# Attention value products as fp32 matmuls in two 64-column halves of TensorE's array

## The chip, the cores and the metric

The kernel runs on one core of a Trainium2 chip. The metric is the device time of one execution in microseconds. Before the change it is 2939.94 us, the median of three runs (2930.49 to 2944.06).

## The reference

One block of a model with 2048 tokens of width 1024, all in fp32. The input is normalised and modulated, projected by `w_in`, and mixed in two ways: an attention with three branches (compressed keys, selected blocks, a window of 512), and a recurrent mixer. Both outputs are normalised and projected back, and a gated feed-forward layer with a short convolution follows. The part that the change touches are the last lines of each attention branch:

```python
o_cmp = jnp.einsum('bgrsc,bgcd->bgrsd', p_cmp.astype(vc.dtype), vc)
...
p = _masked_softmax(jnp.einsum('bgrqd,bgqnd->bgrqn', qb, kg) * scale, mask)
return jnp.einsum('bgrqn,bgqnd->bgrqd', p.astype(vg.dtype), vg)
...
o_win = jnp.einsum('bgrnqk,bgnkd->bgrnqd', p_w.astype(vband.dtype), vband).reshape(B, G, R, S, DH)

g = jax.nn.sigmoid(zg + gate_b).reshape(B, S, G, R, N_BRANCH).transpose(0, 2, 3, 1, 4)
o = g[..., 0:1] * o_cmp + g[..., 1:2] * o_slc + g[..., 2:3] * o_win
```

There are 2 groups of keys and values, 4 query heads for each group, and 64 columns for each head. Queries go in blocks of 128.

## The kernel before

The kernel has three stages, each with pools of its own. The first projects the input in four chunks of 512 tokens, runs the recurrent mixer and writes queries, keys and values to DRAM. The second is the attention with the output projection. The third is the feed-forward layer, again in four chunks.

Most products are made in fp32r with both operands split: a tile is copied to an fp32r tile "h" (on ScalarE), and what is left of it goes into a second tile "l" (a subtraction, mostly on VectorE). A product is then three matmuls: h by h, h by l, l by h (`mm3`).

The attention stage runs over units, one for each query tile `i` (16 of them, in the order of `TILES`) and group `g`. `score_steps` makes the scores of the next unit and their exponentials, scaled by the gates; the tile `pc` holds the compressed and the window branch, the tiles `ps` the selected one. `value_steps` makes the value product of the current unit. Its work is a list of jobs, one for each tile of up to 128 keys: one job for the compressed keys (8 for each query tile up to the current one, so 8 to 128 rows), up to five for the window, and one for each tile of the selected branch, so that a unit has 3 to 22 jobs.

For each job, `flip` turns the four heads' weights around with four transposes on TensorE (line 785) into a PSUM tile `pt`, copies it to the fp32r tile `th` on ScalarE (line 786) and puts the rest into `tl` on VectorE (line 787). The values are stored split as well: 64 columns of "h" and 64 of "l" side by side, so one stationary tile of 128 columns. Two matmuls of 512 columns (lines 796 and 797) accumulate the job into `po`, whose lower 64 partitions collect the products with the values' h and whose upper 64 those with l:

```python
                pe.matmul(po, jobs[n][1], th, start=(n == 0), stop=False)
                pe.matmul(po, jobs[n][1], tl, start=False, stop=(n == N - 1))
```

`LOOK = 4` jobs are flipped ahead of the one that is multiplied. At the end of a unit the two halves of `po` are copied out on ScalarE (lines 805 and 806) and added on GpSimd (line 811).

Python's `weave` interleaves the steps of the value product, the next unit's scores and the previous tile's output projection (`project_steps`, line 131). The order of the instructions that the engines get is then set by the framework's scheduler, which goes by a timeline of its own (`schedule_with_timeline_sim=True`). Each engine runs its own stream in the order in which it was built, and waits on semaphores.

Two other places of the first stage speak of the same kind of arithmetic and matter for the trace: `ada_product` (line 173) multiplies in plain fp32 into four strips of 32 columns of the array, and the compressed keys (`pk`, line 545) are an fp32 product with 64 stationary columns and 256 streamed.

Of the kernel before, what the change touches and what calls it, by code (L numbers as in the profile page):

```python
# [9 lines left out]
F32 = mybir.dt.float32  # L10
F32R = mybir.dt.float32r
AF = mybir.ActivationFunctionType
OP = mybir.AluOpType
AX = mybir.AxisListType

P = 128
# [5 lines left out]
NQ = S // P  # L22
FF = 2816
NF = FF // P
G, R, DH = 2, 4, 64
# [18 lines left out]
LOOK = 4  # L44
# [9 lines left out]
def hymba_block(ctx, tc, x, vecs, rows, ada, w_in, w_v, lru_w, cmp_w1, cmp_w2, w_out, w_gu, w_dn,  # L54
# [6 lines left out]
    cst = ctx.enter_context(tc.tile_pool(name="cst", bufs=1))  # L61
# [2 lines left out]

    Q_d = dr.tile([G, DH, 2, R, S], F32, name="Q_d")
    K_d = dr.tile([2, G, 2, DH, S], F32, name="K_d")
    V_d = dr.tile([2, P, NQ, G, P], F32, name="V_d")
    C_d = dr.tile([2, G, 16, DH, S // 16], F32, name="C_d")
    L_d = dr.tile([P, 2, 4, S], F32, name="L_d")
    KC_d = dr.tile([G, 2, DH, P], F32, name="KC_d")  # L70
# [31 lines left out]
    gates = cst.tile([P, NQ, 24], F32, name="gates")  # L102

    rlru = cst.tile([P, NQ], F32, name="rlru")
    VC = cst.tile([P, G, P], F32R, name="VC")
    cvec = cst.tile([P, 8], F32, name="cvec")

    def reserve(pl, *tags):
# [111 lines left out]
    with tc.tile_pool(name="a", bufs=1, reuse_waits="tile") as pl, tc.tile_pool(name="ap", bufs=1, space=PSUM, reuse_waits="tile") as pp:  # L220
# [109 lines left out]
        def chunk(c, hT):  # L330
# [116 lines left out]
            def v_tiles(each=None):  # L447

                wv = [weights(c, "v", hf) for hf in range(2)]
                zv = [pp.tile([P, 280], F32, name=f"zv{c}_{t}", tag="z", bufs=4) for t in range(4)]  # L450
                for k in range(KT):
                    for t in range(4):
                        sl = slice(t * P, (t + 1) * P)
                        mm3(zv[t], [((hT[k][0][:, sl], hT[k][1][:, sl]),
                                     (wv[k // 4][0][:, k % 4], wv[k // 4][1][:, k % 4]))], 3 * k, 24)
                    if each:
                        each(k)
                for t in range(4):
                    ps = zv[t]
                    st = pl.tile([P, 4, 2, DH], F32R, name=f"vs{c}_{t}", tag="vst", bufs=2)  # L460
                    psv = ps[:, 0:256].rearrange("p (b d) -> p b d", d=DH)
                    act.activation(st[:, :, 0, :], psv, AF.Copy)
                    dve.tensor_tensor(st[:, :, 1, :], psv, st[:, :, 0, :].bitcast(F32), op=OP.subtract)
                    dve.tensor_tensor(gates[:, 4 * c + t, :], ps[:, 256:280], gb, op=OP.add)
                    sync.dma_start(V_d[:, :, 4 * c + t].rearrange("n p g d -> p n (g d)"),
                                   st.rearrange("p (n g) l d -> p n (g l d)", n=2).bitcast(F32))

            def zs(js):
                for j in js:
# [44 lines left out]
        def compress_step(q):  # L514
            n, qd = q // 4, q % 4
            if qd == 0:
                cs["ps"] = [pp.tile([P, G, NS], F32, name=f"ph{n}{hf}", tag="z", bufs=4) for hf in range(2)]
            wh, wl = weights(NCH - 1, "c", q)
            xh = pl.tile([P, 4, G, P], F32R, name=f"xbh{q}", tag="x", bufs=4)
            xl = pl.tile([P, 4, G, P], F32R, name=f"xbl{q}", tag="x", bufs=4)  # L520
            o = VEC["pos"][0] + 16 * n + 4 * qd
            pos = vec[:, o:o + 4].unsqueeze(2)
            a = int(qd < 2)
            for g in range(G):
                f = cs[q][g]
                dve.tensor_tensor(f[:, :, a:P], f[:, :, a:P], pos.to_broadcast([P, 4, P - a]), op=OP.add)
                act.activation(xh[:, :, g, :], f, AF.Copy)
                dve.tensor_tensor(xl[:, :, g, :], f, xh[:, :, g, :].bitcast(F32), op=OP.subtract)
            if q < 7:
                compress_load(q + 1)  # L530
            for hf in range(2):
                sl = slice(hf * P, (hf + 1) * P)
                mm3(cs["ps"][hf], [((wh[:, m, sl], wl[:, m, sl]), (xh[:, m], xl[:, m])) for m in range(4)], 12 * qd, 48)
            if qd < 3:
                return
            hid = []
            for hf in range(2):
                h = pl.tile([P, G, NS], F32, name=f"hid{n}{hf}", tag="xsh", bufs=2)
                dve.tensor_scalar(h, cs["ps"][hf], V("cb1", 2 * n + hf), None, op0=OP.add)
                gelu_tail(h, h, pl, [P, G, NS], "ge", True)  # L540
                hid.append(h)
            if n == 0:
                pk = pp.tile([DH, G * NS], F32, name="pk", tag="g", bufs=2)
                for hf in range(2):
                    pe.matmul(pk, w2[:, 0, hf, :], hid[hf].rearrange("p g s -> p (g s)"), start=(hf == 0), stop=(hf == 1))
                kf = pl.tile([DH, G, NS], F32, name="kf", tag="ge", bufs=2)
                b2 = V("cb2k")[0:DH]
                dve.tensor_scalar(kf, pk.rearrange("p (g s) -> p g s", g=G), b2, None, op0=OP.add)
                kh = pl.tile([DH, 2, G, NS], F32R, name="kh", tag="vst", bufs=2)
                act.activation(kh[:, 0], kf, AF.Copy)  # L550
                dve.tensor_tensor(kh[:, 1], kf, kh[:, 0].bitcast(F32), op=OP.subtract)
                for g in range(G):
                    act.dma_start(KC_d[g].rearrange("l d s -> d l s"), kh[:, :, g, :].bitcast(F32))
            else:
                pv = pp.tile([P, G, DH], F32, name="pv", tag="g", bufs=2)
                for g in range(G):
                    for hf in range(2):
                        pe.matmul(pv[:, g], hid[hf][:, g, :], w2[:, 1, hf, :], start=(hf == 0), stop=(hf == 1))
                vf = pl.tile([P, G, DH], F32, name="vf", tag="ge", bufs=2)
                dve.tensor_tensor(vf, pv, cb2v.unsqueeze(1).to_broadcast([P, G, DH]), op=OP.add)  # L560
                act.activation(VC[:, :, 0:DH], vf, AF.Copy)
                dve.tensor_tensor(VC[:, :, DH:P], vf, VC[:, :, 0:DH].bitcast(F32), op=OP.subtract)


        hT, wts = [], []
# [54 lines left out]
    with tc.tile_pool(name="t", bufs=1, reuse_waits="tile") as pl, tc.tile_pool(name="tp", bufs=1, space=PSUM, reuse_waits="tile") as pp:  # L620
        reserve(pp, ("s", 4096, 2), ("pt", 2048, 3), ("o", 2048, 1))
        reserve(pl, ("MW", 2560, 1), ("ci", 4 * CW, 2), ("Q", 4096, 2), ("K", 3072, 2), ("ks", 2048, 4),
                ("pc", 12288, 2), ("ps", 4096, 10), ("V", 2560, 2), ("vs", 2048, 3), ("pth", 2048, 4),
                ("ptl", 2048, 4))
        MW = pl.tile([P, 640], F32, name="MW", tag="MW", bufs=1)
        sync.dma_start(MW, mask_w)
        wo = {}
# [132 lines left out]
        def value_steps(i, g, u):  # L760

            nw, nk = u["nw"], i + 1
            Vt = pl.tile([P, 5, P], F32R, name=f"V{i}_{g}", tag="V", bufs=2)
            sync.dma_start(Vt[:, 0:nw].bitcast(F32), V_d[1, :, i + 1 - nw:i + 1, g, :])
            jobs = []
            C = 8 * nk
            jobs.append((lambda h: u["pc"][:, h, 0:C], VC[0:C, g, :]))
# [1 line left out]
                jobs.append((lambda h, j=j: u["pc"][:, h, C + j * P:C + (j + 1) * P], Vt[:, j, :]))  # L769
            for a in range(0, nk, 4):  # L770
                n = min(4, nk - a)
                vt = pl.tile([P, 4, P], F32R, name=f"vs{i}_{g}_{a}", tag="vs", bufs=3)
                sync.dma_start(vt[:, 0:n].bitcast(F32), V_d[0, :, a:a + n, g, :])
                for j in range(n):
                    jobs.append((lambda h, a=a, j=j: u["ph"][h][a // 8][:, (a % 8 + j) * P:(a % 8 + j + 1) * P], vt[:, j, :]))
            po = pp.tile([P, 512], F32, name=f"po{i}_{g}", tag="o", bufs=1)

            def flip(n):
                pt = pp.tile([P, 512], F32, name=f"pt{i}_{g}_{n}", tag="pt", bufs=3)
                th = pl.tile([P, 512], F32R, name=f"th{i}_{g}_{n}", tag="pth", bufs=4)  # L780
                tl = pl.tile([P, 512], F32R, name=f"tl{i}_{g}_{n}", tag="ptl", bufs=4)
                K = jobs[n][1].shape[0]
                pt, th, tl = pt[0:K], th[0:K], tl[0:K]
                for h in range(R):
                    pe.transpose(pt[:, h * P:(h + 1) * P], jobs[n][0](h), ident)  # L785
                act.activation(th, pt, AF.Copy)  # L786
                dve.tensor_tensor(tl, pt, th.bitcast(F32), op=OP.subtract)  # L787
                return th, tl

            N = len(jobs)  # L790
            fl = {n: flip(n) for n in range(min(LOOK, N))}
            for n in range(N):
                if n + LOOK < N:
                    fl[n + LOOK] = flip(n + LOOK)
                th, tl = fl.pop(n)
                pe.matmul(po, jobs[n][1], th, start=(n == 0), stop=False)
                pe.matmul(po, jobs[n][1], tl, start=False, stop=(n == N - 1))
                yield
            if g == 0:
                out_of[i] = (pl.tile([P, 2, 4, P], F32R, name=f"mx{i}", tag="mx", bufs=1),  # L800
                             pl.tile([P, 4, P], F32, name=f"sq{i}", tag="sq", bufs=1))
# [47 lines left out]
        def ffn_norm(i):  # L849
# [7 lines left out]
            yield  # L857
            for hf in range(2):
                pt = pp.tile([P, 4, P], F32, name=f"ft{i}{hf}", tag="pt", bufs=3)
                h = pl.tile([P, 4, P], F32R, name=f"fh{i}{hf}", tag="pth", bufs=4)  # L860
                l = pl.tile([P, 4, P], F32R, name=f"fl{i}{hf}", tag="ptl", bufs=4)
                f = pl.tile([P, 4, P], F32, name=f"ff{i}{hf}", tag="ps", bufs=10)
                for j in range(4):
                    k = 4 * hf + j
# [214 lines left out]
```

## Time and profile before

| | us |
|---|---|
| median of three runs | 2939.94 |
| profiled execution | 2934.73 |
| its span, first to last instruction | 2933.0 |
| TensorE (PE) busy in it | 2832.0 |
| VectorE (DVE) busy | 1694.0 |
| ScalarE (ACT) busy | 1497.8 |
| GpSimd (POOL) busy | 1322.3 |

The projection stage reaches to about 572 us, the attention stage from there to about 1437, the feed-forward stage from there to the end. Matmuls of a stream overlap, so that the sum of their durations is more than the time that they take; the distance from one start to the next is what one costs.

### The profile page before, as it was taken

The page shows a single profiled execution, that of the slowest core. Times are in us where ns is not written, and L with a number is a line of the kernel's source. Part 1 is how long each engine was busy: PE and PEld are TensorE (multiplying, and loading weights), DVE is VectorE, ACT ScalarE, POOL GpSimd, SP SyncE. Part 2 cuts the span into 40 slices and gives each one's busy share as a digit, 9 for nine tenths or more (in the row PEclk, how much of TensorE's full clock was granted, in tenths as well). Part 3 has the DMA queues.
Part 4 walks back from the last instruction along what each step waited for, and adds up shares of the span by engine and source line. Part 5 has one row for each costly group of instructions (what it writes and reads, how often), then busy time and mean ns, then how long its engine had stood idle before and what let it go on. Part 6 is the DMA issues. An engine that isn't in the chain of part 4 may idle for free. (4 is left out here: it accounts for less than half of the span.)

```text
span 2933.0 us, 40574 instructions
## 1 busy us (share of the span) xinstructions
PE 2832.0 (97%) x14436; PEld 2328.3 (79%) x14436; DVE 1694.0 (58%) x3149; ACT 1497.8 (51%) x2686; POOL 1322.3 (45%) x1392
## 2 busy tenths in 40 slices
PE   8999999889999899999999999999999999999998
PEld 6777778777778777888788888888887888888886
DVE  4656657776777888888566621666216662166610
ACT  5656566586777777777633333433334333233322
POOL 1111010166666556565344445544455444554444
PEclk9999999999999999999999999999999999999999
DMA  7576655764544434433533333433324333243332
GB/s 285 177 268 203 242 196 151 225 164 129 138 137 121 123 111 111 116 110 96 190 94 96 104 118 98 140 99 96 128 86 151 94 103 121 88 135 100 97 105 78
DMA packets 256617, 397.89 MB, mean 136 GB/s; under 512 B 41376, under 2 KB 168352, under 8 KB 256416
## 3 DMA queue, kind: packets, MB, share of 16 engines
q1 hardware_dynamic: 255808, 394.12, 43.5%
q8 instruction: 115, 1.88, 0.3%
q0 software_dynamic: 320, 1.05, 0.1%
q14 instruction: 86, 0.70, 0.1%
q10 hardware_dynamic: 288, 0.13, 0.0%
HBM read 342.15 MB, written 53.08 MB: 135 GB/s over the span
## 5 line engine op out<-in xcount | busy, mean ns | idle before, releaser
L787 DVE TENSOR_TENSOR tl<-pt,th 128x512 fp32r<-128x512 f32 (+4 forms) x444 | 295.2, 684 | 46.9 <-ACT th L786 45.0
L944 DVE TENSOR_SCALAR ac<-gp,vec 128x512 f32<-128x512 f32 x88 | 188.5, 2143 | 215.6 <-ACT gp L941 208.5
L786 ACT ACTIVATE th<-pt 128x512 fp32r<-128x512 f32 (+4 forms) x444 | 255.1, 594 | 103.2 <-PE pt L785 98.4
L976 DVE TENSOR_TENSOR o<-pt,o 128x128 f32<-128x128 f32 x128 | 28.3, 284 | 433.1 <-PE pt L973 433.1
L757 POOL TENSOR_SCALAR ps<-ps,rs,gates 128x1024 f32<-128x1024 f32 (+7 forms) x192 | 182.0, 958 | 160.3 <-DVE rs L754 116.4
L952 DVE TENSOR_TENSOR gl<-ac,gh 128x512 fp32r<-128x512 f32 x88 | 209.5, 2381 | 69.4 <-ACT gh L951 69.4
L947 ACT ACTIVATE ac<-ac 128x512 f32<-128x512 f32 x88 | 55.7, 633 | 310.7 <-DVE ac L946 310.7
L751 ACT ACTIVATE ps<-ps,mn 128x1024 f32<-128x1024 f32 (+7 forms) x192 | 171.5, 897 | 51.6 <-DVE mn L651 51.3
L785 PE MATMUL pt<-ident,ps 128*128 128x128 f32 x1088 | 167.4, 275 | 7.8 <-DVE tl L787 6.5
L785 PEld LDWEIGHTS pt<-ident,ps 128*128 128x128 f32 x1088 | 133.0, 141 | 44.1 <-DVE tl L787 13.0
L124 POOL TENSOR_TENSOR wd_0l<-wd,wd_0h 128x1408 fp32r<-128x1408 f32 x32 | 103.1, 3223 | 139.8 <-ACT wd_0h L123 139.8
L646 PE MATMUL ss<-ks,Q 128*128 128x512 f32 (+3 forms) x640 | 162.2, 374 | 4.0 <-DVE mn L651 2.1
L124 POOL TENSOR_TENSOR wd_1l<-wd,wd_1h 128x1408 fp32r<-128x1408 f32 x32 | 103.2, 3224 | 130.8 <-ACT wd_1h L123 113.7
L946 DVE SCALAR_TENSOR_TENSOR ac<-gp,vec,ac 128x512 f32<-128x512 f32 x176 | 136.3, 774 | 6.1
L131 PE MATMUL pd<-gl,wd_0h 128*128 128x512 f32 x352 | 139.7, 397 | 0.0
L646 PEld LDWEIGHTS ss<-ks,Q 128*128 128x128 f32 x640 | 114.5, 191 | 30.1 <-issue 4.4
L131 PE MATMUL pd<-gh,wd_0h 128*128 128x512 f32 x352 | 137.9, 392 | 0.0
L131 PE MATMUL pd<-gl,wd_1h 128*128 128x512 f32 x352 | 137.7, 391 | 0.0
L131 PE MATMUL pd<-gh,wd_0l 128*128 128x512 f32 x352 | 137.5, 391 | 0.0
L131 PE MATMUL pd<-gh,wd_1l 128*128 128x512 f32 x352 | 137.3, 390 | 0.0
L131 PE MATMUL pd<-gh,wd_1h 128*128 128x512 f32 x352 | 137.2, 390 | 0.0
L123 ACT ACTIVATE wd_0h<-wd 128x1408 fp32r<-128x1408 f32 x32 | 44.2, 1383 | 158.2 <-PE pd L131 99.8
(1557 smaller groups left out, 8621.8 us busy)
## 6 DMA issues: line engine op xcount, KB each, us to landing
wg<-in_w_gu_dram SPq DMA_DIRECT2D x88, 512.0 KB, 3.6
wu<-in_w_gu_dram SPq DMA_DIRECT2D x88, 512.0 KB, 3.6
wd<-in_w_dn_dram SPq DMA_DIRECT2D x64, 704.0 KB, 4.1
wr<-in_w_in_dram SPq DMA_DIRECT2D x64, 512.0 KB, 5.1
ad<-in_ada_dram SPq DMA_DIRECT2D x32, 512.0 KB, 4.8
Q<-Q_d SPq DMA_DIRECT2D x64, 256.0 KB, 4.5
ks<-K_d SPq DMA_DIRECT2D x56, 256.0 KB, 3.4
vs<-V_d SPq DMA_DIRECT2D x56, 256.0 KB, 3.1
```

The source lines that it names most:

```text
L124: (lo_eng or dve).tensor_tensor(l, raw, h.bitcast(F32), op=OP.subtract)
L131: pe.matmul(ps, a, b, start=(n == 0), stop=(n == total - 1))
L646: pe.matmul(ps[:, o:o + W], Qt[:, hl, h * P:(h + 1) * P], K_ap, start=(hl == 0), stop=(hl == 1))
L751: act.activation(p, p, AF.Exp, scale=-1.0, bias=init, accum_out=sm[:, h, 2 + n:3 + n])
L757: pool.tensor_scalar(p, p, rs[:, h, 2:3], gt[:, h, 1:2], op0=OP.mult, op1=OP.mult)
L785: pe.transpose(pt[:, h * P:(h + 1) * P], jobs[n][0](h), ident)
L786: act.activation(th, pt, AF.Copy)
L787: dve.tensor_tensor(tl, pt, th.bitcast(F32), op=OP.subtract)
L944: dve.tensor_scalar(ac, gp[:, 0:TC], V("fcw", f), V("fcb", f), op0=OP.mult, op1=OP.add)
L946: dve.scalar_tensor_tensor(ac, gp[:, k:k + TC], V("fcw", k * NF + f), ac, op0=OP.mult, op1=OP.add)
L947: act.activation(ac, ac, AF.Silu)
L952: dve.tensor_tensor(l, ac, h.bitcast(F32), op=OP.subtract)
```

## The change

The values are no longer split. They are stored as 64 fp32 columns for each group, in DRAM (`V_d`), in the tiles that are loaded for a unit (`Vt`, `vt`), and for the compressed branch (`VC`). The turned weights are copied once, as fp32, in even jobs by ScalarE and in odd jobs by VectorE; the subtraction is gone. A job is one matmul in fp32 with 64 stationary columns: even jobs write the lower 64 partitions of `po`, odd jobs the upper 64, each half of the array with an accumulation of its own. The jobs are taken two at a time: two flips, then two matmuls, then two yields. What is done with the halves of `po` at the end of a unit is unchanged.

```diff
--- before.py
+++ after.py
@@ -64,7 +64,7 @@
 
     Q_d = dr.tile([G, DH, 2, R, S], F32, name="Q_d")
     K_d = dr.tile([2, G, 2, DH, S], F32, name="K_d")
-    V_d = dr.tile([2, P, NQ, G, P], F32, name="V_d")
+    V_d = dr.tile([2, P, NQ, G, DH], F32, name="V_d")
     C_d = dr.tile([2, G, 16, DH, S // 16], F32, name="C_d")
     L_d = dr.tile([P, 2, 4, S], F32, name="L_d")
     KC_d = dr.tile([G, 2, DH, P], F32, name="KC_d")
@@ -102,7 +102,7 @@
     gates = cst.tile([P, NQ, 24], F32, name="gates")
 
     rlru = cst.tile([P, NQ], F32, name="rlru")
-    VC = cst.tile([P, G, P], F32R, name="VC")
+    VC = cst.tile([P, G, DH], F32, name="VC")
     cvec = cst.tile([P, 8], F32, name="cvec")
 
     def reserve(pl, *tags):
@@ -457,13 +457,11 @@
                         each(k)
                 for t in range(4):
                     ps = zv[t]
-                    st = pl.tile([P, 4, 2, DH], F32R, name=f"vs{c}_{t}", tag="vst", bufs=2)
-                    psv = ps[:, 0:256].rearrange("p (b d) -> p b d", d=DH)
-                    act.activation(st[:, :, 0, :], psv, AF.Copy)
-                    dve.tensor_tensor(st[:, :, 1, :], psv, st[:, :, 0, :].bitcast(F32), op=OP.subtract)
+                    st = pl.tile([P, 4, DH], F32, name=f"vs{c}_{t}", tag="vst", bufs=2)
+                    act.activation(st, ps[:, 0:256].rearrange("p (b d) -> p b d", d=DH), AF.Copy)
                     dve.tensor_tensor(gates[:, 4 * c + t, :], ps[:, 256:280], gb, op=OP.add)
                     sync.dma_start(V_d[:, :, 4 * c + t].rearrange("n p g d -> p n (g d)"),
-                                   st.rearrange("p (n g) l d -> p n (g l d)", n=2).bitcast(F32))
+                                   st.rearrange("p (n g) d -> p n (g d)", n=2))
 
             def zs(js):
                 for j in js:
@@ -556,10 +554,7 @@
                 for g in range(G):
                     for hf in range(2):
                         pe.matmul(pv[:, g], hid[hf][:, g, :], w2[:, 1, hf, :], start=(hf == 0), stop=(hf == 1))
-                vf = pl.tile([P, G, DH], F32, name="vf", tag="ge", bufs=2)
-                dve.tensor_tensor(vf, pv, cb2v.unsqueeze(1).to_broadcast([P, G, DH]), op=OP.add)
-                act.activation(VC[:, :, 0:DH], vf, AF.Copy)
-                dve.tensor_tensor(VC[:, :, DH:P], vf, VC[:, :, 0:DH].bitcast(F32), op=OP.subtract)
+                dve.tensor_tensor(VC, pv, cb2v.unsqueeze(1).to_broadcast([P, G, DH]), op=OP.add)
 
 
         hT, wts = [], []
@@ -620,8 +615,7 @@
     with tc.tile_pool(name="t", bufs=1, reuse_waits="tile") as pl, tc.tile_pool(name="tp", bufs=1, space=PSUM, reuse_waits="tile") as pp:
         reserve(pp, ("s", 4096, 2), ("pt", 2048, 3), ("o", 2048, 1))
         reserve(pl, ("MW", 2560, 1), ("ci", 4 * CW, 2), ("Q", 4096, 2), ("K", 3072, 2), ("ks", 2048, 4),
-                ("pc", 12288, 2), ("ps", 4096, 10), ("V", 2560, 2), ("vs", 2048, 3), ("pth", 2048, 4),
-                ("ptl", 2048, 4))
+                ("pc", 12288, 2), ("ps", 4096, 10), ("V", 1280, 2), ("vs", 1024, 3), ("pth", 2048, 8))
         MW = pl.tile([P, 640], F32, name="MW", tag="MW", bufs=1)
         sync.dma_start(MW, mask_w)
         wo = {}
@@ -760,8 +754,8 @@
         def value_steps(i, g, u):
 
             nw, nk = u["nw"], i + 1
-            Vt = pl.tile([P, 5, P], F32R, name=f"V{i}_{g}", tag="V", bufs=2)
-            sync.dma_start(Vt[:, 0:nw].bitcast(F32), V_d[1, :, i + 1 - nw:i + 1, g, :])
+            Vt = pl.tile([P, 5, DH], F32, name=f"V{i}_{g}", tag="V", bufs=2)
+            sync.dma_start(Vt[:, 0:nw], V_d[1, :, i + 1 - nw:i + 1, g, :])
             jobs = []
             C = 8 * nk
             jobs.append((lambda h: u["pc"][:, h, 0:C], VC[0:C, g, :]))
@@ -769,33 +763,36 @@
                 jobs.append((lambda h, j=j: u["pc"][:, h, C + j * P:C + (j + 1) * P], Vt[:, j, :]))
             for a in range(0, nk, 4):
                 n = min(4, nk - a)
-                vt = pl.tile([P, 4, P], F32R, name=f"vs{i}_{g}_{a}", tag="vs", bufs=3)
-                sync.dma_start(vt[:, 0:n].bitcast(F32), V_d[0, :, a:a + n, g, :])
+                vt = pl.tile([P, 4, DH], F32, name=f"vs{i}_{g}_{a}", tag="vs", bufs=3)
+                sync.dma_start(vt[:, 0:n], V_d[0, :, a:a + n, g, :])
                 for j in range(n):
                     jobs.append((lambda h, a=a, j=j: u["ph"][h][a // 8][:, (a % 8 + j) * P:(a % 8 + j + 1) * P], vt[:, j, :]))
             po = pp.tile([P, 512], F32, name=f"po{i}_{g}", tag="o", bufs=1)
 
             def flip(n):
                 pt = pp.tile([P, 512], F32, name=f"pt{i}_{g}_{n}", tag="pt", bufs=3)
-                th = pl.tile([P, 512], F32R, name=f"th{i}_{g}_{n}", tag="pth", bufs=4)
-                tl = pl.tile([P, 512], F32R, name=f"tl{i}_{g}_{n}", tag="ptl", bufs=4)
+                th = pl.tile([P, 512], F32, name=f"th{i}_{g}_{n}", tag="pth", bufs=8)
                 K = jobs[n][1].shape[0]
-                pt, th, tl = pt[0:K], th[0:K], tl[0:K]
+                pt, th = pt[0:K], th[0:K]
                 for h in range(R):
                     pe.transpose(pt[:, h * P:(h + 1) * P], jobs[n][0](h), ident)
-                act.activation(th, pt, AF.Copy)
-                dve.tensor_tensor(tl, pt, th.bitcast(F32), op=OP.subtract)
-                return th, tl
+                if n % 2:
+                    dve.tensor_copy(th, pt)
+                else:
+                    act.activation(th, pt, AF.Copy)
+                return th
+
 
             N = len(jobs)
             fl = {n: flip(n) for n in range(min(LOOK, N))}
-            for n in range(N):
-                if n + LOOK < N:
-                    fl[n + LOOK] = flip(n + LOOK)
-                th, tl = fl.pop(n)
-                pe.matmul(po, jobs[n][1], th, start=(n == 0), stop=False)
-                pe.matmul(po, jobs[n][1], tl, start=False, stop=(n == N - 1))
-                yield
+            for a in range(0, N, 2):
+                for n in range(a + LOOK, min(a + LOOK + 2, N)):
+                    fl[n] = flip(n)
+                for n in range(a, min(a + 2, N)):
+                    o = 64 * (n % 2)
+                    pe.matmul(po[o:o + 64, :], jobs[n][1], fl.pop(n), start=(n < 2), stop=(n + 2 >= N))
+                for n in range(a, min(a + 2, N)):
+                    yield
             if g == 0:
                 out_of[i] = (pl.tile([P, 2, 4, P], F32R, name=f"mx{i}", tag="mx", bufs=1),
                              pl.tile([P, 4, P], F32, name=f"sq{i}", tag="sq", bufs=1))
@@ -857,8 +854,8 @@
             yield
             for hf in range(2):
                 pt = pp.tile([P, 4, P], F32, name=f"ft{i}{hf}", tag="pt", bufs=3)
-                h = pl.tile([P, 4, P], F32R, name=f"fh{i}{hf}", tag="pth", bufs=4)
-                l = pl.tile([P, 4, P], F32R, name=f"fl{i}{hf}", tag="ptl", bufs=4)
+                h = pl.tile([P, 4, P], F32R, name=f"fh{i}{hf}", tag="pth", bufs=8)
+                l = pl.tile([P, 4, P], F32R, name=f"fl{i}{hf}", tag="pth", bufs=8)
                 f = pl.tile([P, 4, P], F32, name=f"ff{i}{hf}", tag="ps", bufs=10)
                 for j in range(4):
                     k = 4 * hf + j
```

The scheduler then orders the instructions of the changed kernel. In the rows below `ptI_g_n` is the PSUM tile of job n of tile I and group g, `thI_g_n` and `tlI_g_n` its copies, and `poI_g` the unit's accumulator; a number behind these only tells buffers apart. The first place is the middle of a unit's value product on TensorE, tile 12, group 1. Before:

```order
L785 MATMUL pt12_1_12_13487<-ident_71,ps12_1_2_0_13199 128x128
L785 MATMUL pt12_1_12_13487<-ident_71,ps12_1_3_0_13241 128x128
L797 MATMUL po12_1_13286<-tl12_1_9_13427,vs12_1_0_13278 128x512
L796 MATMUL po12_1_13286<-th12_1_10_13446,vs12_1_4_13280 128x512
L785 MATMUL pt12_1_13_13505<-ident_71,ps12_1_0_0_13076 128x128
L785 MATMUL pt12_1_13_13505<-ident_71,ps12_1_1_0_13130 128x128
L785 MATMUL pt12_1_13_13505<-ident_71,ps12_1_2_0_13199 128x128
L785 MATMUL pt12_1_13_13505<-ident_71,ps12_1_3_0_13241 128x128
L797 MATMUL po12_1_13286<-tl12_1_10_13447,vs12_1_4_13280 128x512
L796 MATMUL po12_1_13286<-th12_1_11_13457,vs12_1_4_13280 128x512
```

And in the changed kernel:

```order
L778 MATMUL pt12_1_13_12545<-ident_71,ps12_1_1_0_12226 128x128
L778 MATMUL pt12_1_13_12545<-ident_71,ps12_1_2_0_12287 128x128
L778 MATMUL pt12_1_13_12545<-ident_71,ps12_1_3_0_12325 128x128
L793 MATMUL po12_1_12369<-th12_1_10_12503,vs12_1_4_12363 64x512
L778 MATMUL pt12_1_14_12561<-ident_71,ps12_1_0_1_12212 128x128
L778 MATMUL pt12_1_14_12561<-ident_71,ps12_1_1_1_12264 128x128
L778 MATMUL pt12_1_14_12561<-ident_71,ps12_1_2_1_12294 128x128
L778 MATMUL pt12_1_14_12561<-ident_71,ps12_1_3_1_12333 128x128
L793 MATMUL po12_1_12369<-th12_1_11_12510,vs12_1_4_12363 64x512
```

The two matmuls of a job and its neighbour stood next to each other (the rest `tl` of one job, then `th` of the next), with four transposes between such pairs. Now the matmuls of jobs 10 (lower half) and 11 (upper half) each stand alone, with the four transposes of another job on either side.

The second place is near the end of the same value product, again on TensorE. Before:

```order
L797 MATMUL po12_1_13286<-tl12_1_15_13543,vs12_1_8_13282 128x512
L796 MATMUL po12_1_13286<-th12_1_16_13560,vs12_1_8_13282 128x512
L646 MATMUL ss13_0_1_1_13582<-ks13_0_8_13346,Q13_0_13336 128x512 x2
L646 MATMUL ss13_0_1_1_13582<-ks13_0_12_13348,Q13_0_13336 128x256 x2
L646 MATMUL ss13_0_2_0_13607<-ks13_0_0_13342,Q13_0_13336 128x512 x2
L646 MATMUL ss13_0_2_0_13607<-ks13_0_4_13344,Q13_0_13336 128x512 x2
L797 MATMUL po12_1_13286<-tl12_1_16_13561,vs12_1_8_13282 128x512
L796 MATMUL po12_1_13286<-th12_1_17_13571,vs12_1_8_13282 128x512
```

And in the changed kernel:

```order
L778 MATMUL pt12_1_18_12628<-ident_71,ps12_1_3_1_12333 128x128
L793 MATMUL po12_1_12369<-th12_1_15_12569,vs12_1_8_12365 64x512
L793 MATMUL po12_1_12369<-th12_1_16_12599,vs12_1_8_12365 64x512
L778 MATMUL pt13_0_0_12703<-ident_71,pc13_0_12430 112x128 x4
L640 MATMUL ss13_0_1_1_12615<-ks13_0_8_12426,Q13_0_12416 128x512 x2
L640 MATMUL ss13_0_1_1_12615<-ks13_0_12_12428,Q13_0_12416 128x256 x2
L640 MATMUL ss13_0_2_0_12638<-ks13_0_0_12422,Q13_0_12416 128x512 x2
L640 MATMUL ss13_0_2_0_12638<-ks13_0_4_12424,Q13_0_12416 128x512 x2
L793 MATMUL po12_1_12369<-th12_1_17_12606,vs12_1_8_12365 64x512
```

Here jobs 15 and 16 come to stand next to each other, one in each half, while job 17 stands alone behind the next unit's scores.

The third place is ScalarE over the same unit. Before:

```order
L786 ACTIVATE th12_1_7_13386<-pt12_1_7_13385 128x512
L786 ACTIVATE th12_1_8_13406<-pt12_1_8_13405 128x512
L786 ACTIVATE th12_1_9_13426<-pt12_1_9_13425 128x512
L786 ACTIVATE th12_1_10_13446<-pt12_1_10_13445 128x512
L786 ACTIVATE th12_1_11_13457<-pt12_1_11_13456 128x512
L786 ACTIVATE th12_1_12_13488<-pt12_1_12_13487 128x512
```

And in the changed kernel:

```order
L782 ACTIVATE th12_1_6_12444<-pt12_1_6_12443 128x512
L782 ACTIVATE th12_1_8_12469<-pt12_1_8_12468 128x512
L692 ACTIVATE pc13_0_12430,sm13_0_12432<-pc13_0_12430,mn13_0_12431 128x112
L694 ACTIVATE pc13_0_12430,sm13_0_12432<-pc13_0_12430,mn13_0_12431 128x640
L782 ACTIVATE th12_1_10_12503<-pt12_1_10_12502 128x512
L782 ACTIVATE th12_1_12_12539<-pt12_1_12_12538 128x512
L782 ACTIVATE th12_1_14_12562<-pt12_1_14_12561 128x512
```

ScalarE copied every job, and now copies the even ones; the copies of the odd jobs stand in VectorE's stream, between the masked minima of the next unit's scores.

Over the whole stage the changed order holds 444 value matmuls in 348 runs without another matmul between: 263 runs of one, 76 of two, 8 of three and 1 of five. Within a run the halves alternate. 271 runs stand right behind transposes of line 778 (line 785 before), and 192 have such transposes right behind them.

## Rows read from the trace of the kernel before

**Rows 1.** Busy us of each engine (count), granted clock, DMA, by stretch.

```profile
0.00:572.00 572.00, 534.31 (x3256) 434.54 (x3257) 352.70 (x576) 339.86 (x504) 61.15 (x104) 0.99 0.67 218
572.00:672.00 100.00, 84.60 (x436) 66.72 (x436) 74.94 (x263) 73.59 (x198) 64.51 (x113) 0.91 0.60 157
672.00:1437.00 765.00, 737.08 (x4150) 610.19 (x4149) 605.22 (x1684) 562.84 (x1287) 459.07 (x667) 1.00 0.43 122
1437.00:2933.00 1496.00, 1476.01 (x6598) 1216.80 (x6597) 661.17 (x626) 521.51 (x698) 737.59 (x509) 1.00 0.34 110
```

**Rows 2.** Groups from 572 to 1437 us: count | busy, mean ns | idle before, releasers.

```profile
L785 PE MATMUL pt<-ident,ps 128*128 128x128 f32 x1088 | 167.4, 275 | 7.8 <-DVE tl L787 6.5 <-DVE mn L651 0.6 <-DVE rs L754 0.3
L785 PE MATMUL pt<-ident,pc 128*128 128x128 f32 (+9 forms) x688 | 102.6, 275 | 5.8 <-POOL pc L723 2.9 <-POOL pc L725 1.4 <-DVE tl L787 1.2
L786 ACT ACTIVATE th<-pt 128x512 fp32r<-128x512 f32 (+4 forms) x444 | 255.1, 594 | 103.2 <-PE pt L785 98.4 <-DVE mn L651 0.9 <-DVE bi L721 0.3
L787 DVE TENSOR_TENSOR tl<-pt,th 128x512 fp32r<-128x512 f32 (+4 forms) x444 | 295.2, 684 | 46.9 <-ACT th L786 45.0 <-DMA H_d<-fl 0.4
L796 PE MATMUL po<-th,vs 128*128 128x512 f32 x272 | 111.4, 410 | 5.9 <-ACT th L786 5.8
L796 PE MATMUL po<-th,V 128*128 128x512 f32 x140 | 58.5, 418 | 2.0 <-ACT th L786 2.0
L796 PE MATMUL po<-th,VC 40*128 40x512 f32 (+15 forms) x32 | 15.2, 476 | 2.3 <-ACT th L786 1.3 <-ACT o L806 1.1
L797 PE MATMUL po<-tl,vs 128*128 128x512 f32 x272 | 123.3, 453 | 0.8 <-DVE tl L787 0.8
L797 PE MATMUL po<-tl,V 128*128 128x512 f32 x140 | 65.4, 467 | 0.0
L797 PE MATMUL po<-tl,VC 40*128 40x512 f32 (+15 forms) x32 | 13.8, 432 | 0.0
L646 PE MATMUL ss<-ks,Q 128*128 128x512 f32 (+3 forms) x640 | 162.2, 374 | 4.0 <-DVE mn L651 2.1 <-issue 1.1 <-PE sa L646 0.6
L646 PE MATMUL sa<-K,Q 128*128 128x272 f32 (+14 forms) x453 | 95.1, 336 | 11.2 <-DVE mn L651 5.8 <-DMA Q<-Q_d 3.6 <-DVE rs L754 1.5
L131 PE MATMUL p<-wo,lt 128*128 128x512 f32 x373 | 92.8, 398 | 3.4 <-DVE tl L787 3.3
L131 PE MATMUL p<-wo,mx 128*128 128x512 f32 x360 | 87.8, 391 | 0.0
```

**Rows 3.** Timeline of TensorE in the attention stage: start, duration, instructions.

```profile
1274.93 0.60 PE L785 MATMUL pt<-ident,pc 128*128 128x128 f32 x4
1275.29 0.48 PE L797 MATMUL po<-tl,V 128*128 128x512 f32 x1
1275.61 0.40 PE L796 MATMUL po<-th,V 128*128 128x512 f32 x1
...
1304.62 2.92 PE L131 MATMUL p<-wo,lt 128*128 128x512 f32 x12
```

**Rows 4.** Timeline of TensorE around the compressed keys' product in the first stage.

```profile
522.26 0.40 PE L131 MATMUL zk<-hh,w72h 128*128 128x512 f32 x1
522.58 0.65 PE L545 MATMUL pk<-hid,w 128*64 128x256 f32 x2
523.16 0.50 PE L131 MATMUL zk<-hl,w72h 128*128 128x512 f32 x1
523.49 0.39 PE L131 MATMUL zk<-hh,w72l 128*128 128x512 f32 x1
```

**Rows 5.** Timeline of TensorE around one ada product in the first stage.

```profile
208.86 0.40 PE L131 MATMUL zy<-hh,w24l 128*128 128x512 f32 x1
209.19 0.65 PE L173 MATMUL aprb<-ad,caz 128*32 128x128 f32 x16
209.77 0.38 PE L182 MATMUL apc<-ones,adrb 128*128 128x1 f32 x2
```

**Rows 6.** The group of the values' subtraction in the first stage.

```profile
L463 DVE TENSOR_TENSOR vs<-zv,vs 128x256 fp32r<-128x256 f32 x16 | 6.7, 420 | 0.7 <-ACT vs L462 0.6
```

## The prediction

> **What bounds the kernel now.** I read first the busy time by stretch [rows 1]. The attention stage lies between 572 and 1437 us. In it TensorE is busy 84.6 + 737.1 = 821.7 of 865 us, so it stands idle only 43 us; VectorE is busy 680 us, ScalarE 636, GpSimd 524. The projection stage before it and the feed-forward stage after it are bounded by TensorE too, and the change hardly touches them. So a change of the value products is worth what it does to TensorE's time inside this stage, plus whatever part of the 43 us of waiting it gives back.
>
> Next the groups of the stage [rows 2]. A "job" (one tile of keys) is four transposes (1088 + 688 = 1776 of them), a copy on ScalarE (0.594 us), a subtraction on VectorE (0.684 us) and two fp32r matmuls; there are 272 + 140 + 32 = 444 jobs, so 888 value matmuls. The durations of matmuls there are not their price, because they overlap: the price is the distance between starts. For that I read the timeline [rows 3]: twelve fp32r matmuls of 512 columns last 2.92 us, the last of them 0.39, so one every (2.92 - 0.39)/11 = 0.23 us; four transposes last 0.60 us, the last of them 0.27, so one every 0.11. A job therefore costs TensorE 4 x 0.11 + 2 x 0.23 = 0.90 us. The same rows show it in practice: from the transposes at 1274.93 over the two matmuls to 1275.61 + 0.23 is 0.91 us. Going between transposes and fp32r matmuls thus costs nothing that shows.
>
> How much waiting is in the stage beyond the 43 us that the idle time shows? A wait can hide under a matmul's tail. At the price of starts, the stage's matmuls need: value 888 x 0.23 = 204; output projection 733 x 0.23 = 169; transposes 1776 x 0.11 = 195; scores, mean duration less the tail 0.39 - 0.23 = 0.16, 640 x 0.21 + 453 x 0.18 = 217; some 5 for the rest. That is 790 of 865, so waiting and other gaps are at most 75 us and at least 43.
>
> **What the change removes and adds on TensorE.** It removes the 888 fp32r matmuls: 204 us. It adds 444 fp32 matmuls, each 64 columns wide in the array and 512 columns streamed.
>
> What does one cost? The trace has the shape at half the length: the two key products of the compression, 64 columns wide, 256 streamed, fp32 [rows 4]. One such matmul shows as two records. Between the fp32r matmul at 522.26 and the one at 523.49 lie 1.23 us; two of these steps are ordinary (2 x 0.23), so the excursion costs 0.77. Its streaming: the ada products [rows 5] are fp32 in four strips of 32 columns. Sixteen records of 128 columns last 0.65 us, the last 0.27; so three further records in each strip take 0.38, about 0.12 each. An fp32r pass of 128 columns is 0.23/4 = 0.06. So a record is two passes, and an fp32 matmul four. The key product streams 4 x 0.115 = 0.46 us, and 0.77 - 0.46 = 0.31 us is the price of entering and leaving the half array. The rows show where: the step into it takes 0.32 us instead of 0.23, the next fp32r matmul starts 0.58 after the excursion began instead of 0.46, and the one behind that 0.33 later instead of 0.23, with its weight load not hidden. A value matmul standing alone is then 4 x 0.23 + 0.31 = 1.23 us against 0.46 now. Next to transposes, which are themselves paced by their weight loads, one load of 0.11 should not show: 1.12. I use 1.15, nearer the lower bound, because by the built order 271 of the 348 runs come straight behind transposes and 192 are followed by them.
>
> The Trainium skill (TensorEngine Tiling (Array Packing), "Tiling Modes", Key Properties) says that changing the tiling mode drains the engine. It speaks against this change, gives no price, and the trace agrees with it by the 0.31 us.
>
> Two strips stream side by side: in [rows 5] four do. But two value matmuls can share a slot only where they stand next to each other in TensorE's order, and there the built order decides. Even and odd jobs are adjacent in the code; in the order four transposes mostly stand between them, as shown above. Counted over the stage, the 444 matmuls stand in 348 runs: 263 of one, 76 of two, 8 of three, 1 of five. Seven of the runs of two or more begin with the compressed tile at 64 rows or fewer, another array shape, which I count as a run of its own: 355 entries, and 365 slots of 0.92 us. So the stage gets 355 x 1.15 + 10 x 0.92 = 417 us, and loses 204: **+213 us** of TensorE time (bounds +203 at 1.12 and +242 at 1.23).
>
> **What it gives back.** VectorE loses 444 x 0.684 = 304 us and gets 222 copies; a copy from PSUM is bounded by ScalarE's 0.594 below and the subtraction's 0.684 above, so 132 to 152 us. ScalarE loses 222 x 0.594 = 132 us. Both were 74 to 79% busy and fall to some 530 and 505 us in a longer stage, and a transposed tile leaves PSUM after one pass instead of two. TensorE's waits on the copy, on the subtraction and on the score minima should therefore largely go. The bounds are 0 and 75; I take 55, since the jobs' waits are most of the named ones in [rows 2], while the first tiles (572 to 672, granted clock 0.91) also wait for chains of other engines that the change leaves alone.
>
> **At nothing.** The projection stage loses 16 subtractions of 0.42 us on VectorE [rows 6], which is idle for 219 of the 572 us there; were they exposed, 7 us. The compressed values lose two small operations once. The value loads carry half the bytes, at a DMA share of 0.43. The eight copy buffers of one tag take the place of four and four.
>
> Sum: 213 - 55 = +158 us on the profiled 2934.73, so 3093; the median of the runs shown is 5 us above the profiled one, so **3098 us**.
>
> **The rivals.**
> 1. The waits are not given back. TensorE runs its stream in order, and every second tile now waits for VectorE's copy, which can stand behind a masked minimum. For: the built order puts copies there. Against: with a job at 1.6 us of TensorE time and four jobs of look-ahead, a copy has some 6 us. Time: 2940 + 213 to 242 = 3153 to 3182.
> 2. The granted clock falls in the value stage. For: it was 0.91 from 572 to 672. Against: it was 1.00 through the rest, and through the ada products in strips. If the whole longer stage had 0.91, it would be 9% of about 1020 us longer, 92 us: 3190. It decides from a mean below 0.97.
> 3. On the other side: the two halves overlap in spite of the transposes between them, with no drain. Then 222 pairs and 10 odd halves of jobs cost 232 x 0.92 = 213 against 204, the waits come back, and the time is 2940 + 9 - 55 = 2894. It wins from a price per lone matmul below (204 + 55)/365 = 0.71 us; [rows 4] have 0.77 for half the columns, with the fp32r stream stopped on both sides.
> The Trainium skill (TensorE: Matmul & The Clock Gate, Part 3: Packing small matmuls) gives about this: packed tiles cost one matmul's duration plus some 4 ns for each further tile. [Rows 5] bear it out for neighbours; nothing here shows it across a transpose.
> 4. All 75 us of waits go at the lower price: 2940 + 203 - 75 = 3068; this is the near end of the forecast, not a case of its own.
>
> **How the numbers follow.** Forecast (TensorE pays for lone halves, most waits return, 3060 to 3145) 0.70; rival 1, 0.15; rival 2, 0.07; rival 3, 0.04; 0.04 for what I have not thought of, half of it near no change. A measurement of this kernel tells about 0.5% (15 us) from no change. Faster 0.05, same 0.02, slower 0.93. For 8 in 10 the range must hold the forecast and most of rival 1: 3035, which leaves 5% on the price of a run, to 3180.
>
> **What would show it.** Right: 888 records of the value matmul 64 columns wide, a lone one taking 1.1 to 1.2 us from start to start; where two stand together, the second's records start beside the first's; the stage ends near 1590 instead of 1437; VectorE near 530 us and ScalarE near 505 in it; TensorE's idle time under 20 us; granted clock 1.00; the feed-forward stage still 1496 us. Wrong: if records of opposite halves overlap with transposes between them, if a record takes one pass, if TensorE waits for VectorE's copies, or if the clock falls.

## The result, and the profile after

The changed kernel takes 3116.74 us (median of four runs, 3115.46 to 3119.45) against 2941.64 us for the kernel before in the same comparison: a ratio of 1.0612, 95% interval 1.0598 to 1.0626. The time lies 19 us above the forecast of 3098 us and inside its range of 3035 to 3180.

The busy time by stretch, in the columns of [rows 1], with the stage's later end:

```profile
0.00:572.00 572.00, 537.71 (x3252) 437.30 (x3252) 346.27 (x555) 339.18 (x503) 58.65 (x104) 0.98 0.66 214
572.00:672.00 100.00, 90.18 (x433) 58.92 (x433) 59.36 (x231) 64.62 (x178) 56.67 (x101) 0.93 0.55 145
672.00:1616.00 944.00, 929.40 (x4151) 529.88 (x4149) 491.04 (x1489) 469.25 (x1095) 462.60 (x679) 1.00 0.32 88
1616.00:3113.70 1497.70, 1477.77 (x6603) 1217.58 (x6602) 660.88 (x626) 521.07 (x698) 736.76 (x509) 1.00 0.34 108
```

The whole difference lies in the attention stage: 865 us became 1044, the feed-forward stage went from 1496.0 to 1497.7, and the projection stage ends within 1 us of where it did. In the attention stage TensorE is idle for 1044 - 90.2 - 929.4 = 24 us instead of 43, VectorE is busy 550 us instead of 680 and ScalarE 534 instead of 636: lighter engines beside a TensorE that has more to do.

The groups of the stage that answer to [rows 2]:

```profile
L778 PE MATMUL pt<-ident,ps 128*128 128x128 f32 x1088 | 170.8, 280 | 4.4 <-DVE th L780 2.0 <-ACT th L782 1.5 <-POOL ps L751 0.6
L778 PE MATMUL pt<-ident,pc 128*128 128x128 f32 (+10 forms) x688 | 105.3, 282 | 10.4 <-POOL pc L717 4.0 <-POOL pc L719 3.2 <-ACT th L782 2.6
L782 ACT ACTIVATE th<-pt 128x512 f32<-128x512 f32 (+12 forms) x232 | 134.3, 590 | 202.8 <-PE pt L778 201.8
L780 DVE COPY th<-pt 128x512 f32<-128x512 f32 x212 | 145.6, 688 | 145.0 <-PE pt L778 144.4
L793 PE MATMUL po<-th,vs 128*64 128x512 f32 x542 | 243.8, 617 | 0.0
L793 PE MATMUL po<-th,V 128*64 128x512 f32 x280 | 122.2, 617 | 0.0
L793 PE MATMUL po<-th,VC 40*64 40x512 f32 (+15 forms) x64 | 34.2, 616 | 0.0
L640 PE MATMUL ss<-ks,Q 128*128 128x512 f32 (+3 forms) x640 | 174.1, 395 | 4.5 <-DVE mn L645 2.8 <-PE sa L640 1.2
L640 PE MATMUL sa<-K,Q 128*128 128x272 f32 (+14 forms) x457 | 100.5, 345 | 5.1 <-DVE mn L645 4.1 <-DVE rs L748 0.9
```

The value matmuls show 886 of their 888 records here, two for each of 444, now 64 columns wide; the last two start behind 1616 us. They wait for nothing (the 0.0 in the idle column); it is ScalarE and VectorE that wait for the transposes, 202 and 144 us.

TensorE's timeline in the middle of a unit, the counterpart of [rows 3]:

```profile
1366.87 1.08 PE L793 MATMUL po<-th,vs 128*64 128x512 f32 x4
1367.88 0.65 PE L778 MATMUL pt<-ident,ps 128*128 128x128 f32 x4
...
1371.20 1.08 PE L793 MATMUL po<-th,vs 128*64 128x512 f32 x4
1372.21 0.66 PE L778 MATMUL pt<-ident,ps 128*128 128x128 f32 x4
1372.80 1.07 PE L793 MATMUL po<-th,vs 128*64 128x512 f32 x2
1373.80 0.66 PE L778 MATMUL pt<-ident,ps 128*128 128x128 f32 x4
1374.39 1.07 PE L793 MATMUL po<-th,vs 128*64 128x512 f32 x2
```

Read the starts. A lone value matmul (x2, its two records) at 1372.80 is followed by transposes at 1373.80: 1.00 us. Two in opposite halves (x4) at 1371.20 are followed at 1372.21: 1.01 us. From one group of transposes to the next round a lone matmul it is 1373.80 - 1372.21 = 1.59 us, where a job took 0.90 before.

That neighbours in opposite halves start together shows where their tiles have different names, as the compressed one (`VC`) and one of the window (`V`):

```profile
964.14 0.64 PE L793 MATMUL po<-th,VC 72*64 72x512 f32 x1
964.14 0.64 PE L793 MATMUL po<-th,V 128*64 128x512 f32 x1
964.62 0.59 PE L793 MATMUL po<-th,VC 72*64 72x512 f32 x1
964.62 0.59 PE L793 MATMUL po<-th,V 128*64 128x512 f32 x1
965.15 0.66 PE L778 MATMUL pt<-ident,pc 128*128 128x128 f32 x4
...
810.30 1.07 PE L793 MATMUL po<-th,VC 24*64 24x512 f32 x2
811.29 1.07 PE L793 MATMUL po<-th,V 128*64 128x512 f32 x2
812.30 0.33 PE L778 MATMUL pt<-ident,ps 128*128 128x128 f32 x1
```

With 72 rows in the compressed tile, both take 965.15 - 964.14 = 1.01 us together. With 24 rows they follow each other, 0.99 and 1.01 us.

### The profile page after: what moved, and what is told of

It is laid out like the page before. It is cut to its first block, busy times and chain, and to the rows that moved or that the text cites. A ratio compares the mean times of both kernels' runs of the same rounds, so it can differ in the third digit from the quotient of the medians.

```text
span 3113.7 us, 39668 instructions
## 1 busy us (share of the span) xinstructions
PE 3035.1 (97%) x14436; PEld 2243.7 (72%) x14436; DVE 1557.5 (50%) x2900; ACT 1394.1 (45%) x2473; POOL 1314.7 (42%) x1392
## 3 DMA queue, kind: packets, MB, share of 16 engines
q8 instruction: 114, 1.87, 0.2%
## 5 line engine op out<-in xcount | busy, mean ns | idle before, releaser
L793 PE MATMUL po<-th,vs 128*64 128x512 f32 x544 | 244.9, 617 | 0.0
L782 ACT ACTIVATE th<-pt 128x512 f32<-128x512 f32 (+12 forms) x232 | 134.3, 590 | 202.8 <-PE pt L778 201.8
L780 DVE COPY th<-pt 128x512 f32<-128x512 f32 x212 | 145.6, 688 | 145.0 <-PE pt L778 144.4
L778 PEld LDWEIGHTS pt<-ident,ps 128*128 128x128 f32 x1088 | 122.8, 141 | 121.6 <-ACT th L782 31.8
L640 PE MATMUL ss<-ks,Q 128*128 128x512 f32 (+3 forms) x640 | 174.1, 395 | 4.5 <-DVE mn L645 2.8
```

The costliest lines, as they stand in the source:

```text
L640: pe.matmul(ps[:, o:o + W], Qt[:, hl, h * P:(h + 1) * P], K_ap, start=(hl == 0), stop=(hl == 1))
L780: dve.tensor_copy(th, pt)
L793: pe.matmul(po[o:o + 64, :], jobs[n][1], fl.pop(n), start=(n < 2), stop=(n + 2 >= N))
```

## The experiments

Theory A is the forecast's, with 0.85 us for a slot where the forecast had 0.92: each run of value matmuls (matmuls with no other between them) pays some 0.30 us for entering and leaving the half array, each slot in it (one matmul, or two that share the time) four passes, 0.85 us, and the built order decides how many there are. Its rivals are that TensorE waits for copies (B), and that two strips do not stream together (C). Changes in microseconds are differences of medians; ratios are to the kernel before, which was measured along with each set of runs: 2941.64 us beside the changed kernel, 2936.62 beside pairs, fours, whole array and no subtraction, 2941.22 beside the other four. So a difference between two sets is known to some 5 us.

**Pairs held together.** The first matmul of a pair gets a wait on the second one's copy, nothing else changes (`flip` now also returns the copy's instruction, `fl[n][1]`). With `GROUP = 2`, the rest of the diff left out at the dots:

```diff
...
-                for n in range(a, min(a + 2, N)):
+                ms = []
+                for n in range(a, min(a + GROUP, N)):
                     o = 64 * (n % 2)
-                    pe.matmul(po[o:o + 64, :], jobs[n][1], fl.pop(n), start=(n < 2), stop=(n + 2 >= N))
+                    m = pe.matmul(po[o:o + 64, :], jobs[n][1], fl[n][0], start=(n < 2), stop=(n + 2 >= N))
+                    ms.append(m)
+                for n in range(a + 1, min(a + GROUP, N)):
+                    tc.add_manual_dep(ms[0].ins, fl[n][1].ins.name, SYNC, reason="group")
...
```

> The changed kernel with each pair of value matmuls held until both turned tiles are copied, so that the pair stands together in TensorE's order: 235 runs instead of 348 and about 245 slots instead of 365. Theory A (a lone half-array matmul pays four passes, 0.85 us, and every run pays some 0.30 us for entering and leaving the half array): 113 x 0.30 + 120 x 0.85 = 136 us less than the changed kernel, so 2981 us. Rival B (TensorE is late because it waits for copies, which now alternate between two engines): holding a matmul for a second copy adds waits, so 3117 us or more. Rival C (two strips do not stream together at 512 columns): the slots stay 444 x 0.85, and the time is near 3117 + 68 - 34 = 3150 us.

Measured: 2992.83 us, 1.0186 of the kernel before (1.0171 to 1.0201). Of the changed kernel's 175 us, 124 are gone, by a change of order and the wait that brings it about. Theory A said 2981; B and C said no gain. TensorE's stage is lighter in work, not in waiting: from 572 to 1489 us it is busy 890.3 of 917 us, 129 less than in the changed kernel, and idle 27, 2 more. A stretch of the pairs' timeline, where two flips and one pair take turns:

```profile
1181.45 1.08 PE L796 MATMUL po<-th,vs 128*64 128x512 f32 x4
1182.46 1.09 PE L780 MATMUL pt<-ident,ps 128*128 128x128 f32 x8
1183.48 1.08 PE L796 MATMUL po<-th,vs 128*64 128x512 f32 x4
1184.49 0.77 PE L780 MATMUL pt<-ident,ps 128*128 128x128 f32 x5
```

Two jobs take 1183.48 - 1181.45 = 2.03 us here. As two lone jobs they take 2 x 1.59 = 3.18, and before the change they took 1.80.

**Groups of four.** The same with `GROUP = 4`, the first matmul of a group waiting for the other three copies.

> The same with groups of four jobs (two in each half): 120 runs and about 237 slots. Theory A: against the changed kernel 235 x 0.30 less for entries and 128 x 0.85 less for slots, 180 us, so 2937 us, no slower than the kernel before. Rival B: slower than the pairs, since four copies are waited for. Rival C: about 3117 + 68 - 70 = 3115 us.

Measured: 2962.03 us, 1.0077 (1.0062 to 1.0092): 31 us less than the pairs, where 44 were expected, and 25 us above the expectation of 2937. The price of a group is as expected; its eight records last from 1202.93 to the next matmul at 1204.80, 1.87 us for two slots and one entry:

```profile
1202.40 0.60 PE L780 MATMUL pt<-ident,ps 128*128 128x128 f32 x4
1202.93 1.94 PE L796 MATMUL po<-th,vs 128*64 128x512 f32 x8
1204.80 3.24 PE L133 MATMUL p<-wo,mx 128*128 128x512 f32 x13
```

So what is lacking is lost elsewhere in the stage. Part of it is idle time: TensorE is idle for 33 us from 572 to 1455, 9 more than in the changed kernel. Only 1.3 us of that stand before value matmuls, so there is little waiting for a group's copies. The next two runs looked further.

**Groups of six, and groups of four further ahead.** `GROUP = 6` with `LOOK = 5`, and `GROUP = 4` with `LOOK = 7`, both with eleven buffers for the turned tiles.

> Groups of six jobs, eleven buffers for the turned tiles, five jobs ahead: 88 runs, about 236 slots. Theory A: against the groups of four 32 x 0.30 = 10 us less, 2952 us; if the groups of four lose their 25 us against the expectation by waits for the group's copies, sixes lose more, 2965 to 2975 us.

> Groups of four jobs, with eleven buffers and seven jobs ahead instead of eight and four; runs and slots as in the groups of four. If those lost 25 us because a group waits for its copies: 2940 to 2950 us. If they lost it to weight loads that stand clear behind a change of the array's shape, or to the three PSUM tiles that the transposes fill: 2962 us, unchanged.

Measured: sixes 2956.72 us, 1.0055 (1.0040 to 1.0070), 5 us less than fours, where 10 were expected. Fours further ahead: 2970.68 us, 1.0102 (1.0087 to 1.0117), 9 us more than with the shorter look-ahead. The intervals of both overlap with that of the fours, so neither difference is clear. But more copies in hand brought no gain, so waiting for a group's copies is not what costs the groups of four their 25 us; what does was not found. With the longer look-ahead TensorE is idle for 40 us of the stage; 5.8 of them are two single waits for the loads of `K` and `Q`, which the fours do not show.

**Whole array in fp32.** The values get 64 columns of zeros beside them, so that each matmul is 128 columns wide and the half array is never entered (the wider tiles and the zeros left out at the dots):

```diff
...
-                    o = 64 * (n % 2)
-                    pe.matmul(po[o:o + 64, :], jobs[n][1], fl.pop(n), start=(n < 2), stop=(n + 2 >= N))
+                    pe.matmul(po, jobs[n][1], fl.pop(n), start=(n == 0), stop=(n + 1 == N))
...
```

> The changed kernel with the values padded to 128 columns by 64 columns of zeros, so that each value matmul is fp32 on the whole array: no half array is entered, nothing can run side by side, and the order of the stage stays almost the same. Theory A: 444 x 0.85 = 377 us instead of 365 x 0.85 + 355 x 0.30 = 417, so 40 us less than the changed kernel, 3077 us. If the 0.30 us were paid for going between fp32 and fp32r or transposes and not for the half array: about 3117 + 68 = 3185 us.

Measured: 3072.88 us, 1.0462 (1.0445 to 1.0479), 44 us less than the changed kernel (expected 40). The timeline shows what entering and leaving cost, by their absence:

```profile
1373.53 0.60 PE L780 MATMUL pt<-ident,pc 128*128 128x128 f32 x4
1373.97 1.02 PE L794 MATMUL po<-th,V 128*128 128x512 f32 x2
1374.83 0.60 PE L780 MATMUL pt<-ident,pc 128*128 128x128 f32 x4
1375.26 1.02 PE L794 MATMUL po<-th,V 128*128 128x512 f32 x2
```

The transposes take 0.44 us to the next start, the four passes 0.86: 1.30 us a job instead of 1.59, both in fp32 between the same transposes. The 0.29 us are the half array's. So the half array, as the order came out, cost more than it saved.

**One half.** All jobs but the second of each unit go to the lower half: `o = 64 * (n == 1)`, with the flag for the end of an accumulation set accordingly.

> The changed kernel with all value matmuls in the lower half of the array but the second of each unit, so that neighbours cannot stream side by side; 361 runs. Theory A: 444 slots instead of 365, so 79 x 0.85 = 67 us more, and 6 x 0.30 for the runs: 3186 us. If neighbours in different halves did not overlap anyway, the time stays near 3119 us.

Measured: 3169.21 us, 1.0770 (1.0752 to 1.0788), 52 us above the changed kernel where 69 were expected. Neighbours in different halves do stream together, and taking that away costs most of what was reckoned. The expectation counted the compressed tile and the second job of a unit as never overlapping; in the trace they do overlap in 10 of the 32 units, which is 10 x 0.85 = 8.5 us.

**Copies on ScalarE alone.** The `dve.tensor_copy` of odd jobs becomes the activation that even jobs have.

> The changed kernel with all copies of turned tiles on ScalarE, none on VectorE; the arithmetic is the same. The built order comes out with 408 runs of value matmuls instead of 348, and some 417 slots instead of 365. Theory A (runs and slots set the time): 60 x 0.30 + 52 x 0.85 = 62 us more than the changed kernel, 3179 us. Rival B (TensorE waits for VectorE's copies behind the masked minima): up to 20 us less, 3100 us. If neither runs nor copies matter: 3117 us.

Measured: 3160.74 us, 1.0747 (1.0731 to 1.0763), 44 us more than the changed kernel, where 62 were expected. This decides against rival B: VectorE's copies are not what TensorE waits for. Its stage, in the columns of [rows 1], has VectorE lighter by 126 us, ScalarE heavier by 108, and TensorE busy for all but 17 of 1089 us:

```profile
572.00:1661.00 1089.00, 1072.40 (x4589) 596.92 (x4587) 424.07 (x1511) 641.69 (x1487) 518.62 (x779) 0.99 0.34 90
```

The arithmetic is the same. TensorE is busy 53 us longer and idle 7 us less than in the changed kernel, and its trace has 408 runs of value matmuls instead of 348: the order made the difference.

**No subtraction.** The kernel before, with one copy for each job, ScalarE and VectorE in turn, and that copy taken by both matmuls. The remainder of the weights is left out and the product doubled; TensorE's work is that of before. From `flip`:

```diff
...
-                act.activation(th, pt, AF.Copy)
-                dve.tensor_tensor(tl, pt, th.bitcast(F32), op=OP.subtract)
-                return th, tl
+                if n % 2:
+                    dve.tensor_copy(th, pt)
+                else:
+                    act.activation(th, pt, AF.Copy)
+                return th, th
...
```

> The kernel before, with the same 888 fp32r value matmuls on the whole array, but the remainder of the turned weights left out: each job is copied once, by ScalarE or VectorE in turn, and both matmuls take that copy (so the product is doubled and not exact). It shows alone what the lighter VectorE and ScalarE give back. Theory A as forecast: 55 us less than the kernel before, 2886; by what the changed stage left (213 - 179): 34 us less, 2907. Rival: nothing, 2941, if the waits in the stage come from the scores' chain alone.

Measured: 2912.17 us, 0.9914 (0.9899 to 0.9928): 24 us less. Its stage takes 842 us instead of 865, with VectorE at 550 us instead of 680:

```profile
572.00:1414.00 842.00, 813.35 (x4583) 678.93 (x4581) 550.10 (x1717) 527.85 (x1274) 521.32 (x779) 0.99 0.47 129
```

The relief is real, and in this kernel less than half of what the forecast gave for it.

## Why the prediction was right, point by point

**The direction, and where.** Right: all of it lies in the attention stage, because TensorE bounds that stage and the change puts work on it.

**The price of a lone matmul: 1.15 us.** Right between transposes: a job round a lone matmul takes 1.59 us, less 0.44 for the transposes is 1.15. The two parts held less well than their sum. The forecast had 0.92 for four passes and 0.20 for entering and leaving (0.31 less a weight load of 0.11 that would not show), so 1.12, and rounded up; the whole-array run has 0.86 and 0.29. Where fp32r matmuls follow, as behind most of the 156 runs that no transposes follow, it is some 0.05 us more:

```profile
1423.20 1.07 PE L793 MATMUL po<-th,vs 128*64 128x512 f32 x2
1424.21 1.19 PE L640 MATMUL ss<-ks,Q 128*128 128x512 f32 x4
1425.24 0.60 PE L778 MATMUL pt<-ident,ps 128*128 128x128 f32 x4
1425.77 1.07 PE L793 MATMUL po<-th,vs 128*64 128x512 f32 x2
```

The four scores take 1425.24 - 1424.21 = 1.03 us to the next start, 0.11 more than 4 x 0.23. Of the 0.59 us of four transposes between two lone matmuls some 0.06 are for leaving; the other 0.09, for entering again, stand in 1425.77 - 1425.24 = 0.53 here.

**The order decides, not the code.** Right, and the largest point: holding pairs together took away 124 of 175 us, and copies on another engine, which moved the order, added 44 with no more waiting.

**Neighbours share a slot.** Right: 1.01 us for two against 1.00 for one. The Trainium skill (TensorE: Matmul & The Clock Gate, Part 3: Packing small matmuls) gives one matmul's duration and some 4 ns for each further tile; the trace agrees to within its rounding. Rival 3 took two tiles to overlap in this way where they are not neighbours too, and there they did not. The forecast's exception held as well: in all seven runs with a compressed tile of 64 rows or fewer that tile takes its 1.00 us alone, and in the six with more rows it shares.

**The sum of TensorE's work: +213 us.** About right. With 1.20 us for the 163 entries that transposes do not follow, 1.15 for 192, and 10 slots of 0.86, the value matmuls need by estimate 425 us instead of the forecast's 417, so +221. TensorE's busy time rose by 1019.6 - 821.7 = 198 us; it counts waits hidden under a matmul's tail as busy, so part of what came back is in it too.

**What comes back: 55 us.** Wrong in size. The stage grew by 179 us, so with a price of 221 some 42 came back: 19 in idle time, the other 23 a remainder that no row shows. The run without the subtraction measures 24 us, but on the kernel before, where a job takes 0.90 us and not 1.59; with 24 the price would be 203. No run tells the two apart. Either way 55 was too much, and [rows 2] gave it little ground: of the 43 us of idle time there, 21 are waits for the copy (`th`) and the subtraction (`tl`), and 8.5 for the minima (`mn`). In the changed kernel the copies' waits are down to some 6 us of 24, but the minima's are still 7; among the rest are waits for GpSimd's scaled weights and the first tiles, whose clock is 0.93. Price and relief together came out at 179 us in the stage where the forecast had 158, and that is why it was 19 us too low.

**The signs.** The records, the shared starts, the clock and the feed-forward stage came out as forecast. Four marks were missed: the stage ends at 1616 us and not near 1590, VectorE is busy 550 us in it and not 530, ScalarE 534 and not 505, and TensorE is idle 24 us and not under 20.

**At nothing.** Right: VectorE lost 6.4 us in the projection stage and the stage did not move. The DMA share fell from 0.43 to 0.32 behind 672 us, mostly because the stretch is longer: 0.43 x 765 = 329 and 0.32 x 944 = 302 us of transfers, so 27 less. A copy took VectorE 0.688 us, just above the upper of the two bounds. The jobs split into 232 and 212, not two times 222, since a unit with an odd count has one more even job; this changed no term by more than 7 us.

**The rivals.** Waits for copies instead (1): value matmuls wait 0.0 us, and the copies' own run decides against it. The clock (2): 0.93 and 1.00 by stretch against 0.91 and 1.00 before. Overlap across transposes (3): a lone matmul at 1.15 us against the 0.71 from which it would have won.

No version here beats the kernel before with all of its products: the best order tried, groups of six, stays 0.55% above it. The run that is below it leaves the remainder out.

## What to carry to other kernels

Two halves of the array help only where their matmuls are neighbours in the order that the engine gets. Look at the built order before counting on the pairing in the code, and give the scheduler a reason to keep a group together: waits for the whole group's inputs, put on its first matmul, were enough here. Price a change of the array's shape for each run, not for each matmul, and let a run be long. And price the relief of engines that are not the bound by the waits that the profile traces to them: here those were 21 us, and the run that relieved the engines alone gave back 24.

## What the runs showed of the hardware that was not expected

Two fp32 matmuls in opposite halves stream together although each consists of two records: the records start in turn, two at 964.14 and two at 964.62 us, and four records of 512 columns take 1.01 us to the next start, two 1.00. They did not where one had 8 to 64 rows and the other 128: there each took its 1.00 us, in 16 of the 32 units of the pairs' trace, while in the 16 units with 72 rows or more they shared. Entering and leaving the half array cost the same 0.3 us whether one matmul stood in it or eight records did: eight took 1.87 us, which is 1.00 and one slot of 0.86 more, to within 0.01.
